# A batched matrix product: rounding x to float16 first and transposing it on TensorE as float32 words of two values

## Chip, cores and metric

One core of one Trainium2 chip. The metric is the device time in microseconds of one execution; "span" is the part of it that the profile covers (134.7 us of some 136.2).

## The reference

```python
batch, dim_i, dim_j, dim_k = 32, 256, 512, 384      # x: (32,256,512), y: (32,512,384), float32
def reference(x, y):
    return np.einsum('bij,bjk->bik', x, y).astype(np.float32)
```

## The kernel before

Four batches (Q = 4) form a group. A group of x arrives in one load of 2 MB, y and the output move per batch (768 KB and 384 KB). All loads and stores are issued by SyncE (SP) in program order. The multiplies of this kernel take x transposed, so it transposes x on TensorE first (256 transposes, 43.4 us of TensorE's busy time). It is transposed as float32 into PSUM (where this kernel's matrix products and transposes are written), and the eviction, the copy from there to SBUF (where its loaded tiles lie), rounds it to float16. A "bank" is in this text one PSUM tile of the transposes, `t_ps`, with 512 float32 words in each of 128 rows. y is rounded by ScalarE (ACT) and VectorE (DVE).

```python
    def transpose(q):                       # one group of four batches
        x_sb = x_of.pop(q)                  # [128, R=8 rows, J=512] float32
        xt_of[q] = xt_pool.tile([P, Q, NJ, NI, PQ, Q], MM_DT, name="xt_sb")
        n = 0
        for t in range(NJ):                 # NJ = 4
            for e in range(NI):             # NI = 2: eight PSUM banks per group
                t_ps = tpsum_pool.tile([P, Q, Q, PQ], F32, name="t_ps")
                for h in range(Q):          # four transposes fill one bank
                    keep(nc.tensor.transpose(
                            t_ps[:, h].rearrange("c g p -> c (g p)"),
                            x_sb[:, h * NI + e, t::NJ], identity))
                dst = xt_of[q][:, :, t, e].rearrange("c g p h -> c h g p")
                if n % 2 == 0: keep(nc.vector.tensor_copy(dst, t_ps))
                else:          keep(nc.scalar.copy(dst, t_ps))
                n += 1
    # ... load(b), round_y(b): 4 casts of 128x384, multiply(b): 8 matmuls, collect(b): 2 copies, store(b)
    for s in range(B + 2):
        if s + ahead < B:        load(s + ahead)
        if s >= 2:               collect(s - 2)
        if 1 <= s <= B:          multiply(s - 1)
        if s < B and s % Q == 0: transpose(s // Q)
        if s < B:                round_y(s)
        if s >= 2:               store(s - 2)
```

## Time and profile before

| | before |
|---|---|
| time, median of 4 runs (range) | 136.2 us (136.08 to 136.44) |
| bytes moved by the queue | 54.53 MB, 97.9% of the 16 DMA engines' span |
| TensorE / VectorE / ScalarE busy | 66% / 55% / 59% |
| last load of x lands, last eviction of its transposes ends | 115.2 us, 123.2 us |
| last store issued, span | 129.6 us, 134.7 us |

A busy share is an average over the whole span. What counts is the wait that ends last, so the prediction reads the transfer row and then the last 20 us.

### The profile page before, as it was taken

To read this page: it belongs to the slowest core of one execution; us is meant where nothing else is said; L and a number is where in the kernel's file an instruction comes from. 1 tells how busy PE (TensorE), PEld (TensorE's weight loads), DVE (VectorE), ACT (ScalarE), POOL (GpSimd) and SP (SyncE) were. 2 spreads that over 40 slices of the span, in tenths; PEclk is the share of its full clock that TensorE was granted. 3 is DMA by queue.
4 is the path that set the end of the run, shared out by engine and by line. 5 is a ranking of instruction groups with operands and counts; after the bars stand their busy time and mean duration, and the time that the engine had idled before them with its cause. 6 is when DMAs were issued, how large, how long until landed. Compare 5 with 4: busy or idle time off the path is not lost.

```text
span 134.7 us, 1539 instructions
## 1 busy us (share of the span) xinstructions
PE 89.5 (66%) x512; PEld 66.6 (49%) x512; DVE 73.7 (55%) x128; ACT 80.1 (59%) x129; POOL 0.7 (1%) x6
## 2 busy tenths in 40 slices
PE   0049499769677908949794983949459492794920
PEld 0048368644564408925492543936259360793510
DVE  0008855975397503873489340796228870378720
ACT  3007994996299602795479650699218990179910
POOL 2000000000000000000000000000000000000000
PEclk9999999999999985686999599599995999559995
DMA  5999999999999999999999999999999999999992
GB/s 131 399 413 423 447 412 416 416 434 414 404 422 451 425 399 424 421 435 437 400 416 430 438 425 410 421 418 454 407 409 425 433 440 402 421 421 413 412 410 84
DMA packets 10375, 54.62 MB, mean 405 GB/s; under 512 B 1152, under 2 KB 1152, under 8 KB 9344
## 3 DMA queue, kind: packets, MB, share of 16 engines
q1 hardware_dynamic: 10368, 54.53, 97.9%
q8 instruction: 4, 0.07, 0.2%
q14 instruction: 3, 0.02, 0.0%
HBM read 41.94 MB, written 12.58 MB: 405 GB/s over the span
## 4 chain that ended last, share of the span: by engine, by line
DMA 79%; PE 8%; ACT 5%; DVE 2%; issue 2%; SPq 1%; DVEq 0%
DMA y_sb<-in_y_dram 30%; DMA x_sb<-in_x_dram 27%; DMA out_dram<-o_sb 21%; PE o_ps L115 4%; PE t_ps L84 4%; ACT xt_sb L94 2%; ACT y_r L102 2%; DVE xt_sb L92 1%; DVE y_r L104 1%; DVE o_sb L130 0%; SPq L69 0%; ACT o_sb L128 0%; SPq L63 0%; DVEq L130 0%
## 5 line engine op out<-in xcount | busy, mean ns | idle before, releaser
L94 ACT CAST xt_sb<-t_ps 128x512 f16<-128x512 f32 x32 | 39.8, 1350 | 44.0 <-PE t_ps L84 43.9
L92 DVE CAST xt_sb<-t_ps 128x512 f16<-128x512 f32 x32 | 40.1, 1323 | 40.3 <-PE t_ps L84 40.2
L84 PE MATMUL t_ps<-identity,x_sb 128*128 128x128 f32 x256 | 43.4, 340 | 24.5 <-DMA x_sb<-in_x_dram 24.3
L115 PE MATMUL o_ps<-y_r,xt_sb 128*128 128x384 f16 x256 | 46.3, 342 | 14.9 <-ACT y_r L102 14.9
L84 PEld LDWEIGHTS t_ps<-identity,x_sb 128*128 128x128 f32 x256 | 41.1, 216 | 27.8 <-issue 26.4
L115 PEld LDWEIGHTS <-xt_sb 128*128 128x128 f16 x256 | 26.2, 102 | 34.2 <-issue 19.9
L102 ACT CAST y_r<-y_sb 128x384 f16<-128x384 f32 x64 | 30.2, 527 | 0.6 <-DMA y_sb<-in_y_dram 0.6
L130 DVE COPY o_sb<-o_ps 128x384 f32<-128x384 f32 x32 | 17.8, 556 | 15.1 <-PE o_ps L115 15.1
L104 DVE CAST y_r<-y_sb 128x384 f16<-128x384 f32 x64 | 19.9, 354 | 0.4 <-DMA y_sb<-in_y_dram 0.4
L128 ACT COPY o_sb<-o_ps 128x384 f32<-128x384 f32 x32 | 15.4, 483 | 3.8 <-PE o_ps L115 3.8
L94 ACT ACT_TABLE_LOAD x1 | 1.3, 1283 | 0.7 <-PEq L168 0.7
masks.py:199 POOL TENSOR_SCALAR_AFFINE_SELECT identity<-identity 128x128 f32<-128x128 f32 x1 | 0.3, 294 | 0.1
masks.py:197 POOL MEMSET identity<- 128x128 f32 x1 | 0.2, 205 | 0.3 <-POOLq L168 0.3
L168 POOL MEMSET const-bfloat16-1.0<- 128x1 bf16 x1 | 0.1, 102 | 0.0
L168 POOL MEMSET const-uint8-127<- 128x1 uint8 x1 | 0.1, 102 | 0.0
L168 POOL MEMSET const-float32-0.0<- 128x1 f32 x1 | 0.1, 99 | 0.2 <-issue 0.2
L168 POOL MEMSET const-float32-1.0<- 128x1 f32 x1 | 0.1, 99 | 0.0
## 6 DMA issues: line engine op xcount, KB each, us to landing
y_sb<-in_y_dram SPq DMA_DIRECT2D x32, 768.0 KB, 15.1
x_sb<-in_x_dram SPq DMA_DIRECT2D x8, 2048.0 KB, 14.2
out_dram<-o_sb SPq DMA_DIRECT2D x32, 384.0 KB, 14.1
```

What stands on the lines that cost most here:

```text
L84: nc.tensor.transpose(t_ps[:, h].rearrange("c g p -> c (g p)"), x_sb[:, h * NI + e, t::NJ], identity,)
L92: keep(nc.vector.tensor_copy(dst, t_ps))
L94: keep(nc.scalar.copy(dst, t_ps))
L102: keep(nc.scalar.copy(yr_of[b][:, t], y_sb[:, t]))
L104: keep(nc.vector.tensor_copy(yr_of[b][:, t], y_sb[:, t]))
L115: nc.tensor.matmul(ps_of[b][e], xt_sb[:, t, e].rearrange("c p h -> c (p h)"), y_r[:, t], start=(t == 0), stop=(t == NJ - 1),)
L128: keep(nc.scalar.copy(o_of[b][:, e], ps_of[b][e]))
L130: keep(nc.vector.tensor_copy(o_of[b][:, e], ps_of[b][e]))
L168: nc = _bacc.Bacc("TRN2", target_bir_lowering=False, num_devices=1)
```

## The change

The intent is to halve the transposes. x is rounded to float16 before it is transposed, and two neighbouring float16 values are taken together as one 32-bit word for TensorE's transpose. One transpose then carries two values per word, so a group needs 16 transposes instead of 32 and four PSUM banks instead of eight. A bank now holds 1024 values, and VectorE and ScalarE each evict half of it. The layout of the transposed x changes so that the two values of a word, and the four rows h, lie next to each other, and the multiply reads its weights with a step of two values.

```diff
         x_sb = x_of.pop(q)
-        xt_of[q] = xt_pool.tile([P, Q, NJ, NI, PQ, Q], MM_DT, name="xt_sb")
-        ... (32 transposes of x_sb, eight evictions, each of a whole bank, by the engines in turn)
+        x_r = xr_pool.tile([P, R, J], MM_DT, name="x_r")
+        for k in range(0, R, 2):
+            if k % 4 == 0:
+                keep(nc.vector.tensor_copy(x_r[:, k : k + 2], x_sb[:, k : k + 2]))
+            else:
+                keep(nc.scalar.copy(x_r[:, k : k + 2], x_sb[:, k : k + 2]))
+        x_w = x_r.bitcast(F32)
+        xt_of[q] = xt_pool.tile([P, NW, NI, Q * PQ, Q, 2], MM_DT, name="xt_sb")   # NW = 2
+        for n in range(NW):
             for e in range(NI):
-                ...
+                t_ps = tpsum_pool.tile([P, Q, Q * PQ], F32, name="t_ps")
                 for h in range(Q):
+                    keep(nc.tensor.transpose(t_ps[:, h], x_w[:, h * NI + e, n::NW], identity))
+                src = t_ps.bitcast(MM_DT).rearrange("c h (p w) -> c p h w", w=2)
+                half = slice(0, Q // 2), slice(Q // 2, Q)
+                dst = xt_of[q][:, n, e]
+                keep(nc.vector.tensor_copy(dst[:, :, half[0]], src[:, :, half[0]]))
+                keep(nc.scalar.copy(dst[:, :, half[1]], src[:, :, half[1]]))
 ... multiply(b):
-                        xt_sb[:, t, e].rearrange("c p h -> c (p h)"),
+                        xt_sb[:, t // 2, e, own, :, t % 2].rearrange("c p h -> c (p h)"),
```

More of the change, by code (lines that the diff above doesn't have):

```diff
@@ L40 @@
     PQ = P // Q
+    NW = NJ // 2
     const_pool = ctx.enter_context(tc.tile_pool(name="const", bufs=1))
     x_pool = ctx.enter_context(tc.tile_pool(name="x_pool", bufs=3))
+    xr_pool = ctx.enter_context(tc.tile_pool(name="xr_pool", bufs=2))
     y_pool = ctx.enter_context(tc.tile_pool(name="y_pool", bufs=10))
@@ L76, in transpose @@
         x_sb = x_of.pop(q)
-        xt_of[q] = xt_pool.tile([P, Q, NJ, NI, PQ, Q], MM_DT, name="xt_sb")
-        n = 0
-        for t in range(NJ):
+        x_r = xr_pool.tile([P, R, J], MM_DT, name="x_r")
[7 more added lines that the diff above has]
+        for n in range(NW):
             for e in range(NI):
-                t_ps = tpsum_pool.tile([P, Q, Q, PQ], F32, name="t_ps")
+                t_ps = tpsum_pool.tile([P, Q, Q * PQ], F32, name="t_ps")
                 for h in range(Q):
-                    keep(
-                        nc.tensor.transpose(
-                            t_ps[:, h].rearrange("c g p -> c (g p)"),
-                            x_sb[:, h * NI + e, t::NJ],
-                            identity,
-                        )
-                    )
-                dst = xt_of[q][:, :, t, e].rearrange("c g p h -> c h g p")
-                if n % 2 == 0:
-                    keep(nc.vector.tensor_copy(dst, t_ps))
-                else:
-                    keep(nc.scalar.copy(dst, t_ps))
-                n += 1
+                    keep(nc.tensor.transpose(t_ps[:, h], x_w[:, h * NI + e, n::NW], identity))
[4 more added lines that the diff above has]
+                keep(nc.scalar.copy(dst[:, :, half[1]], src[:, :, half[1]]))
     def round_y(b):
@@ L106, in multiply @@
     def multiply(b):
-        xt_sb, y_r = xt_of[b // Q][:, b % Q], yr_of.pop(b)
+        xt_sb, y_r = xt_of[b // Q], yr_of.pop(b)
+        own = slice(b % Q * PQ, (b % Q + 1) * PQ)
         ps_of[b] = [
```

## The prediction

> **What bounds the kernel now.** I read the page first, for the busy shares and the transfer row, and then the last 20 us of the timeline, because a change of compute can only show at the end of a kernel that is bound by transfers.
>
> ```profile
> PE 89.5 (66%) x512; PEld 66.6 (49%) x512; DVE 73.7 (55%) x128; ACT 80.1 (59%) x129; POOL 0.7 (1%) x6
> ...
> DMA  5999999999999999999999999999999999999992
> ...
> q1 hardware_dynamic: 10368, 54.53, 97.9%
> ...
> HBM read 41.94 MB, written 12.58 MB: 405 GB/s over the span
> ...
> DMA y_sb<-in_y_dram 30%; DMA x_sb<-in_x_dram 27%; DMA out_dram<-o_sb 21%; PE o_ps L115 4%; PE t_ps L84 4%; ACT xt_sb L94 2%; ACT y_r L102 2%; DVE xt_sb L92 1%; DVE y_r L104 1%; DVE o_sb L130 0%; SPq L69 0%; ACT o_sb L128 0%; SPq L63 0%; DVE
> ```
>
> No compute engine is busy for more than two thirds of the span. The 16 DMA engines are full in every slice but the first and the last, and the chain that ended last is 79% transfers by its engine line (30 + 27 + 21 in the lines shown, rounded). The 54.53 MB are inputs and outputs that every version has to move (41.94 MB in, 12.58 MB out). At the 413 to 430 GB/s that most middle slices show they need 127 to 132 us of the 134.7 us span.
>
> Next come the groups that the change touches, with the rounding of y as a yardstick for a plain cast:
>
> ```profile
> L94 ACT CAST xt_sb<-t_ps 128x512 f16<-128x512 f32 x32 | 39.8, 1350 | 44.0 <-PE t_ps L84 43.9
> L92 DVE CAST xt_sb<-t_ps 128x512 f16<-128x512 f32 x32 | 40.1, 1323 | 40.3 <-PE t_ps L84 40.2
> L84 PE MATMUL t_ps<-identity,x_sb 128*128 128x128 f32 x256 | 43.4, 340 | 24.5 <-DMA x_sb<-in_x_dram 24.3
> ...
> L102 ACT CAST y_r<-y_sb 128x384 f16<-128x384 f32 x64 | 30.2, 527 | 0.6 <-DMA y_sb<-in_y_dram 0.6
> L130 DVE COPY o_sb<-o_ps 128x384 f32<-128x384 f32 x32 | 17.8, 556 | 15.1 <-PE o_ps L115 15.1
> L104 DVE CAST y_r<-y_sb 128x384 f16<-128x384 f32 x64 | 19.9, 354 | 0.4 <-DMA y_sb<-in_y_dram 0.4
> L128 ACT COPY o_sb<-o_ps 128x384 f32<-128x384 f32 x32 | 15.4, 483 | 3.8 <-PE o_ps L115 3.8
> ```
>
> The evictions of the transposes idle for 40 us and more waiting for TensorE, and TensorE's transposes idle for 24 us waiting for x. That is slack, not cost: the whole line waits for transfers.
>
> The tail is where it could matter. The last group of x lands at 115.2 us. From the timeline of before:
>
> ```profile
> 115.29 6.61 PE L84 MATMUL t_ps<-identity,x_sb 128*128 128x128 f32 x32 [3.29 <-DMA x_sb<-in_x_dram]
> ...
> 120.69 2.55 ACT L94 CAST xt_sb<-t_ps 128x512 f16<-128x512 f32 x2 [0.40 <-PE t_ps L84]
> ...
> 123.61 5.36 PE L115 MATMUL o_ps<-y_r,xt_sb 128*128 128x384 f16 x32 [1.70 <-ACT y_r L102]
> ...
> 129.00 0.56 DVE L130 COPY o_sb<-o_ps 128x384 f32<-128x384 f32 x1 [0.74 <-PE o_ps L115]
> ```
>
> So x(7) takes 8.0 us from landing to its last eviction (115.2 to 123.24), the four batches multiply in 5.36 us, and the last copy ends at 129.56, with its store issued at 129.63. Is the transfer queue waiting for that store, or the store for the queue? The windows of the last microseconds answer it:
>
> ```profile
> 129.00:130.00 1.00, 0.00 (x0) 0.00 (x0) 0.56 (x1) 0.32 (x1) 0.00 (x0) 1.00 1.01 406
> 130.00:131.00 1.00, 0.00 (x0) 0.00 (x0) 0.00 (x0) 0.00 (x0) 0.00 (x0) 1.00 1.01 402
> 131.00:132.00 1.00, 0.00 (x0) 0.00 (x0) 0.00 (x0) 0.00 (x0) 0.00 (x0) 0.74 0.77 307
> 132.00:133.00 1.00, 0.00 (x0) 0.00 (x0) 0.00 (x0) 0.00 (x0) 0.00 (x0) 0.50 0.29 117
> ```
>
> The last two columns are DMA share and GB/s. At 129.63, the bytes still to move are 0.37 x 406 + 402 + 307 + 117 + 12 = 988 KB, of which the last store is 393 KB. So 595 KB, 1.4 us at 420 GB/s, lay ahead of it. The first load was issued at 0.74 us, and bytes flowed from about 1.5 us (213 KB in the second microsecond), so a store needs some 0.7 us to start. The slack of the last store is then about 1.4 - 0.7 = 0.7 us. If the tail's compute ends later than now by d, the kernel ends later by about d - 0.7. If it ends earlier, the gain is at most the half-empty 131 to 133 us: 307 + 117 KB took 2 us where full speed needs 1.0[...]. I put the most to be gained at 0.5 us.
>
> [...]today's evictions write single 2-byte values 8 bytes apart and take 1323 ns for 512 columns, while the contiguous copies from PSUM take 556 ns for 384. [...]in the tail the transposes run at a granted clock of 0.50 up to about 121 us and the multiplies at 1.00. In the group at 73.52 us the 32 multiplies took 6.99 us, because the first 11 started 0.32 us apart instead of 0.16.
>
> **The change part by part, per group of four batches.**
> - *Removed:* 16 of 32 transposes. In the tail 32 took 6.61 us, so 16 take 3.3 us at 0.21 us each. They lie beside other work except in the tail.
> - *Added:* four casts of 128x1024, two on each engine, between the landing of x and the transposes. Scaled from y's casts, VectorE needs at most 354 x 1024/384 = 944 ns and ScalarE at most 527 x 1024/384 = 1405 ns. Both are upper bounds[...]. Two on ScalarE are at most 2.8 us; I expect 2.0 us. This lies on the tail's path.
> - *Changed:* still eight evictions of 512 values each, now two halves of four banks. The writes become runs of four 2-byte values (8 bytes). If this gives the pace of the plain copies from PSUM, they cost at most 556 x 512/384 = 741 ns on VectorE and 644 ns on ScalarE, instead of 1323 and 1350. The reads now hop 512 bytes after each pair, which no row of before prices. I expect 0.6 to 0.75 us.
> - *Changed:* the multiply loads weights with a step of two values. I expect no cost: the loads hide behind multiplies, which are 0.16 us apart.
> - *Unmoved:* every transfer, its size and its order in the queue.
>
> Busy time per group: VectorE 73.7/8 = 9.2 us, less 4 x 1.32, plus 4 x 0.74, plus 2 x 0.94, is 8.8 us. ScalarE 10.0 us, less 5.4, plus 2.6, plus 2.8, is 10.0 us. One group's transfers (6.82 MB at 420 GB/s) take 16.2 us. So in the steady part nothing changes.
>
> The tail: x lands at 115.2, casts end at 117.2 (at most 118.0). The first bank is full 1.14 us later, as now (115.29 to 116.43): 118.4 (119.2). Three more banks follow at TensorE's pace of 0.85 us: 120.9 (121.7). The last bank is evicted by VectorE and then, if they must take turns, by ScalarE: 0.74 + 0.64 more, 122.3 (123.1). Today it is 123.24. The sum is a tail 0.1 to 0.9 us shorter, which is worth 0 to 0.5 us at the end.
>
> **The rivals.**
> 1. *The clock is cold.* Half as many transposes may not wake TensorE before the last multiplies. Then 5.36 us becomes about 7.0 us, as at 73.52: 1.6 us more. With the shorter tail that is 0.7 to 1.5 us late, less the slack of 0.7: +0 to +0.8 us, about 136.6. For it: activity falls from 6.6 to some 3.5 us.[...] I give it two in five.
> 2. *The evictions stay slow* (1.3 us, because of the hops in the read, in turns on each bank). Then the tail's evictions end at 119.2 + 4 x 1.35 + 1.32 = 125.9, 2.7 us late, and the end moves by 2.0 us: 138.2. With a cold clock too, 139.8.[...] Against it: the data move in whole words, in runs. One in eight.
> 3. *TensorE or the evictions limit the kernel now*, so that halving the transposes pays some per cent. The page speaks against it: DMA is full in 38 slices of 40. Below one in fifty.
>
> **Range and chances.** The likeliest end is where it is now: the gain of up to 0.5 us and the cold clock's loss of up to 0.8 us about cancel, so 136.2 us. The low end takes the whole gain and a little noise, 135.5; the high end most of rival 2, 137.8. To be over 2% slower the time must pass 138.9, which needs rival 2 with a cold clock: 6%. Over 2% faster is below 133.4 us, less than the transfers take: 1%. Within 2%: 93%.
>
> **What would show it right or wrong.** DMA share still 97 to 98% with 54.53 MB; 128 transposes instead of 256, with about 22 us of TensorE's busy time gone; x casts near 0.7 us (VectorE) and 1.05 us (ScalarE); evictions under 0.85 us; the last store issued between 128 and 131 us. The prediction is wrong if slices in the middle fall below full DMA (compute then starves the queue), if evictions exceed 1 us, or if the last store is issued after 132 us.

The tail's evictions came to 122.3 us (at most 123.1) against 123.24, so 0.1 to 0.9 us shorter, worth 0 to 0.5 us; against that stood rival 1's loss of up to 0.8 us; together 136.2 us. Rival 1 and rival 2: their chances, two in five and one in eight, were my estimates.

Estimates of mine were also the 2.0 us for two casts on ScalarE and the paces of 0.7 and 1.05 us (under the 944 and 1405 ns scaled from y's casts), the lower end of 0.6 us for an eviction (under the 741 ns scaled from the plain copies), that the two engines might have to take turns on a bank, and that TensorE's clock follows how long it has worked. On the last, the trace of before shows only this: in the tail the granted clock was 0.50 up to 121.0 us, 0.77 from 121.0 to 121.5 and 1.00 from 121.5 to 122.0, all while transposes ran. That casts scaled by their size are upper bounds no view of before shows, but the runs do: x's casts are 2.67 times as large as y's and took 1.95 times as long on VectorE (689 against 354 ns) and 1.98 times on ScalarE (1043 against 527).

## The result, and the profile after

The changed kernel takes 136.2 us (median of 4 runs, 136.06 to 136.40), the kernel before 136.2 us. The outputs are right. The ratio is 0.9999, with a 95% interval of 0.998 to 1.0018. Ratios here are the mean time of one kernel's fast runs over that of the other's of the same rounds, so they are not quite the ratio of the medians.

From the page of the changed kernel: busy shares, transfer row, and the groups that the change touched. The lines of before stand in the prediction.

```profile
PE 78.7 (58%) x384; PEld 50.8 (38%) x384; DVE 58.2 (43%) x144; ACT 75.7 (56%) x145; POOL 0.7 (1%) x6
...
DMA  5999999999999999999999999999999999999992
...
q1 hardware_dynamic: 10368, 54.53, 98.1%
...
L93 PE MATMUL t_ps<-identity,x_r 128*128 128x128 f32 x128 | 29.8, 402 | 33.0 <-DVE x_r L84 31.1
...
L86 ACT CAST x_r<-x_sb 128x1024 f16<-128x1024 f32 x16 | 15.9, 1043 | 28.4 <-DMA x_sb<-in_x_dram 28.2
L98 ACT COPY xt_sb<-t_ps 128x512 f16<-128x512 f16 x32 | 18.3, 587 | 12.9 <-DVE xt_sb L97 12.8
...
L84 DVE CAST x_r<-x_sb 128x1024 f16<-128x1024 f32 x16 | 10.3, 689 | 30.0 <-DMA x_sb<-in_x_dram 30.0
...
L97 DVE COPY xt_sb<-t_ps 128x512 f16<-128x512 f16 x32 | 13.6, 425 | 18.2 <-PE t_ps L93 17.9
```

In a group's line the columns are busy us, mean ns of one, then idle us before the group and what ended most of it. All compute engines have less to do: VectorE 15.5 us less, TensorE 10.8, ScalarE 4.4. The evictions fell from 1323 to 425 ns (VectorE) and from 1350 to 587 ns (ScalarE). The transfer row is the same to the byte. The idle times name the reason: VectorE and ScalarE spent 30 and 28 us waiting for x to land before they could round it. The work that was saved became waiting for transfers.

The tail of the changed kernel, from its timeline:

```profile
114.82 1.99 ACT L86 CAST x_r<-x_sb 128x1024 f16<-128x1024 f32 x2 [3.07 <-DMA x_sb<-in_x_dram]
...
115.67 1.00 PE L93 MATMUL t_ps<-identity,x_r 128*128 128x128 f32 x3 [2.96 <-DVE x_r L84]
...
116.87 2.94 PE L93 MATMUL t_ps<-identity,x_r 128*128 128x128 f32 x13 [0.20 <-ACT x_r L86]
...
120.31 0.58 ACT L98 COPY xt_sb<-t_ps 128x512 f16<-128x512 f16 x1 [0.16 <-DVE xt_sb L97]
...
121.36 4.06 PE L119 MATMUL o_ps<-y_r,xt_sb 128*128 128x384 f16 x24 [1.54 <-ACT y_r L105]
...
125.18 0.93 ACT L105 CAST y_r<-y_sb 128x384 f16<-128x384 f32 x2 [0.68 <-DMA y_sb<-in_y_dram]
...
127.25 0.56 DVE L134 COPY o_sb<-o_ps 128x384 f32<-128x384 f32 x1 [0.93 <-PE o_ps L119]
...
127.87 0.33 SPq L139 DMA_DIRECT2D out_dram<-o_sb  x1
```

From the landing of x to the last eviction it is now 6.1 us (114.82 to 120.89) where it was 8.0. The halved transposes account for it: they run from 115.67 to 119.81, 4.1 us instead of 6.6, while the first casts put 0.85 us in front. The multiplies run at full clock (granted 1.00 in the windows from 120 to 128 us). The last batch even has to wait for its y to land (125.18), and the last store is issued at 127.87 instead of 129.63, 1.8 us earlier. The windows of the end (last columns: granted clock, DMA share, GB/s) show what became of these 1.8 us:

```profile
129.00:130.00 1.00, 0.00 (x0) 0.00 (x0) 0.00 (x0) 0.00 (x0) 0.00 (x0) 0.90 1.05 416
130.00:131.00 1.00, 0.00 (x0) 0.00 (x0) 0.00 (x0) 0.00 (x0) 0.00 (x0) 0.50 1.01 402
131.00:132.00 1.00, 0.00 (x0) 0.00 (x0) 0.00 (x0) 0.00 (x0) 0.00 (x0) 0.50 0.76 304
132.00:133.00 1.00, 0.00 (x0) 0.00 (x0) 0.00 (x0) 0.00 (x0) 0.00 (x0) 0.50 0.34 135
```

These are nearly the rates of before: 416, 402, 304 and 135 against 406, 402, 307 and 117. I call the two half-empty microseconds from 131 to 133 the taper. The engines are idle for the last 7 us, and the queue drains as it did.

### The profile page after: what moved, and what is told of

It reads as the page before. It is cut to its first block, busy times and chain, and to the rows that moved or that the text cites. A ratio compares the mean times of both kernels' runs of the same rounds, so it can differ in the third digit from the quotient of the medians.

```text
span 134.6 us, 1310 instructions
## 1 busy us (share of the span) xinstructions
PE 78.7 (58%) x384; PEld 50.8 (38%) x384; DVE 58.2 (43%) x144; ACT 75.7 (56%) x145; POOL 0.7 (1%) x6
## 3 DMA queue, kind: packets, MB, share of 16 engines
q1 hardware_dynamic: 10368, 54.53, 98.1%
## 4 chain that ended last, share of the span: by engine, by line
DMA 89%; ACT 2%; SPq 2%; PE 1%; issue 0%; DVE 0%; ACTq 0%
DMA y_sb<-in_y_dram 34%; DMA out_dram<-o_sb 31%; DMA x_sb<-in_x_dram 24%; SPq L72 1%; ACT x_r L86 1%; PE o_ps L119 1%; DVE o_sb L134 0%; ACT y_r L105 0%; SPq L66 0%; SPq L139 0%; ACTq L105 0%
## 5 line engine op out<-in xcount | busy, mean ns | idle before, releaser
L119 PE MATMUL o_ps<-y_r,xt_sb 128*128 128x384 f16 x256 | 48.8, 351 | 15.5 <-ACT y_r L105 15.4
L93 PE MATMUL t_ps<-identity,x_r 128*128 128x128 f32 x128 | 29.8, 402 | 33.0 <-DVE x_r L84 31.1
L119 PEld LDWEIGHTS <-xt_sb 128*128 128x128 f16 x256 | 27.0, 105 | 37.2 <-DVE o_sb L134 12.4
L93 PEld LDWEIGHTS t_ps<-identity,x_r 128*128 128x128 f32 x128 | 24.1, 216 | 38.8 <-issue 33.2
L105 ACT CAST y_r<-y_sb 128x384 f16<-128x384 f32 x64 | 29.7, 517 | 4.6 <-DMA y_sb<-in_y_dram 4.6
L86 ACT CAST x_r<-x_sb 128x1024 f16<-128x1024 f32 x16 | 15.9, 1043 | 28.4 <-DMA x_sb<-in_x_dram 28.2
L98 ACT COPY xt_sb<-t_ps 128x512 f16<-128x512 f16 x32 | 18.3, 587 | 12.9 <-DVE xt_sb L97 12.8
L84 DVE CAST x_r<-x_sb 128x1024 f16<-128x1024 f32 x16 | 10.3, 689 | 30.0 <-DMA x_sb<-in_x_dram 30.0
L97 DVE COPY xt_sb<-t_ps 128x512 f16<-128x512 f16 x32 | 13.6, 425 | 18.2 <-PE t_ps L93 17.9
```

The lines of the kernel that those rows point to most:

```text
L84: keep(nc.vector.tensor_copy(x_r[:, k : k + 2], x_sb[:, k : k + 2]))
L86: keep(nc.scalar.copy(x_r[:, k : k + 2], x_sb[:, k : k + 2]))
L93: keep(nc.tensor.transpose(t_ps[:, h], x_w[:, h * NI + e, n::NW], identity))
L97: keep(nc.vector.tensor_copy(dst[:, :, half[0]], src[:, :, half[0]]))
L98: keep(nc.scalar.copy(dst[:, :, half[1]], src[:, :, half[1]]))
L105: keep(nc.scalar.copy(yr_of[b][:, t], y_sb[:, t]))
```

## The experiments

Two questions stayed. Is the change worth anything on the engines, and which part of it? And how much later or earlier may the tail's compute end before the time moves? The first was asked with "light" kernels. They load only three groups of x and eight batches of y and use them again, so their results are wrong, and 25 MB are left to move. The edit, made to the kernel before and to the changed one:

```diff
-        if b % Q == 0:
+        if b % Q == 0 and b // Q < 3:
             x_of[b // Q] = x_pool.tile(...)          # and its load
+        if b >= 8:
+            return
         y_of[b] = y_pool.tile(...)                   # and its load
-        x_sb = x_of.pop(q)
+        x_sb = x_of[q % 3]
-        y_sb = y_of.pop(b)
+        y_sb = y_of[b % 8]
```

### light_before and light_after

> Wrong results on purpose: only the first three x tiles and the first eight y tiles are loaded and then used again; every store stays. 25 MB are left to move instead of 54.5, some 60 us at 420 GB/s, so the engines should set the time. Theory (transfers hide the change): the kernel gets much faster than 136 us, about 100 to 110 us (per group of four batches some 5.5 us of transposes and evictions, 1 us of rounding, 5.4 us of multiplies, 12 us in all, eight times, plus start and end), because nothing but transfers held it at 136. Rival (the engines also hold it near 136 us, so that transfers and engines are about balanced): over 125 us.

> The changed kernel with the same cut in loads (wrong results on purpose). Theory: the change does make the engines' work shorter, and only the transfers hide it, so this beats light_before by about 10 to 15% (90 to 95 us): 2.0 us of casts added, 2 to 3 us of transposes and about 3 us of evictions saved per group. Rival (gain and cost of the change cancel on the engines themselves, and hiding has nothing to do with it): within 2% of light_before.

Measured: light_before 111.9 us (110.44 to 112.0), ratio to the kernel before 0.818 (interval 0.813 to 0.824). light_after 99.98 us (99.23 to 101.63), ratio 0.733 (0.728 to 0.739). Their quotient is 0.733/0.818 = 0.896. The change makes the engines' work 10% shorter once transfers no longer hide it, at the near end of what was expected; the estimate of light_after's time (90 to 95 us) was too low. Both rivals fall: the engines alone need 112 us, not 136, and gain and cost don't cancel on them. From TensorE's timelines, one group's multiplies, the next group's transposes, and its multiplies:

```profile
52.80 5.36 PE L117 MATMUL o_ps<-y_r,xt_sb 128*128 128x384 f16 x32 [1.85 <-ACT y_r L104]
58.00 4.46 PE L86 MATMUL t_ps<-identity,x_sb 128*128 128x128 f32 x32
64.31 5.36 PE L117 MATMUL o_ps<-y_r,xt_sb 128*128 128x384 f16 x32 [1.85 <-ACT y_r L104]
```

```profile
48.59 5.36 PE L121 MATMUL o_ps<-y_r,xt_sb 128*128 128x384 f16 x32 [1.57 <-ACT y_r L107]
53.99 2.78 PE L95 MATMUL t_ps<-identity,x_r 128*128 128x128 f32 x16
58.34 5.36 PE L121 MATMUL o_ps<-y_r,xt_sb 128*128 128x384 f16 x32 [1.57 <-ACT y_r L107]
```

The first fence is light_before: 11.5 us per group. The second is light_after: 9.75 us. The multiplies take 5.36 us in both; the transposes shrink from 4.46 to 2.78 us and the wait before the multiplies from 1.85 to 1.57. What held light_before up can be read from the chain of work that ended last (58 to 82 us): 45% of it are multiplies, 34% VectorE's evictions, and only 6% transposes. In light_after (48 to 69 us) 84% of the chain is ScalarE's work. One group's transfers take 16.2 us (6.82 MB at 420 GB/s). At this pace the engines had 4.7 us of slack per group before, and have 6.4 after. That is where the gain went: off the path, into slack that was there already. In the full kernels I estimate the slack to be smaller: their mean granted clock is 0.89 and 0.83, against 0.999 and 0.982 in these two profiles, and some groups' 32 multiplies took 6.99 and 7.04 us (before) and 6.74 to 7.25 us (after) instead of 5.36.

### light_f16x32: round first, but no pairs

```diff
+    identity_h = const_pool.tile([P, P], MM_DT); nc.vector.tensor_copy(identity_h, identity)
+        x_r = ...                                    # the four casts of the change
-                t_ps = tpsum_pool.tile([P, Q, Q, PQ], F32, name="t_ps")
+                t_ps = tpsum_pool.tile([P, Q, Q, PQ], MM_DT, name="t_ps")
-                            x_sb[:, h * NI + e, t::NJ], identity,
+                            x_r[:, h * NI + e, t::NJ], identity_h,
```

> Half of the change alone, with the cut loads (wrong results on purpose): x is rounded first, but transposed as 32 transposes of single float16 values per group, into float16 PSUM tiles, and evicted with the old scattered writes. If what makes the evictions cheap is the run of adjacent values that pairing allows, evictions stay near 1.3 us and this is slower than light_before by the casts, 5 to 15%. If it is the 16-bit source alone, evictions fall to about 0.5 us and this is near light_after.

Measured: 125.8 us (123.55 to 127.16; two of the four runs count as slow, the fast ones took 123.55 and 125.28), ratio of the fast runs to the kernel before 0.913 (0.905 to 0.920), so 0.913/0.818 = 1.115 times light_before: 11.5% slower. Its profile was taken in a slow run, so I use only its durations, beside those of light_before's profile, which was a fast run. light_f16x32, then light_before:

```profile
L103 DVE COPY xt_sb<-t_ps 128x512 f16<-128x512 f16 x32 | 38.0, 1334 | 6.6 <-PE t_ps L95 6.6
L105 ACT COPY xt_sb<-t_ps 128x512 f16<-128x512 f16 x32 | 38.2, 1387 | 4.7 <-PE t_ps L95 4.7
```

```profile
L96 ACT CAST xt_sb<-t_ps 128x512 f16<-128x512 f32 x32 | 38.7, 1394 | 24.3 <-PE t_ps L86 24.3
...
L94 DVE CAST xt_sb<-t_ps 128x512 f16<-128x512 f32 x32 | 38.7, 1344 | 20.7 <-PE t_ps L86 20.7
```

A 16-bit source makes the evictions no cheaper at all (1334 against 1344 ns, 1387 against 1394). Rounding first, alone, is a loss. But the casts are not shown to be its cause, as I had expected. From TensorE's timeline of the same profile:

```profile
43.76 7.04 PE L126 MATMUL o_ps<-y_r,xt_sb 128*128 128x384 f16 x32 [2.21 <-ACT y_r L113]
...
57.47 7.48 PE L126 MATMUL o_ps<-y_r,xt_sb 128*128 128x384 f16 x32 [1.70 <-ACT y_r L113]
```

A group takes 13.7 us, 2.2 more than in light_before, and the multiplies, partly at half clock, take 1.7 to 2.1 of them: from 57.47 us the first 13, by their weight loads, start 0.32 us apart, as in the kernel before from 73.5 to 76.7 us, where the granted clock was 0.50. The fast runs have no profile; their mean granted clock (0.88 and 0.90, against 0.96 to 1.00 in light_before) points the same way.

### light_scatter: pairs, but the old writes

```diff
-        xt_of[q] = xt_pool.tile([P, NW, NI, Q * PQ, Q, 2], MM_DT, name="xt_sb")
+        xt_of[q] = xt_pool.tile([P, NW, NI, 2, Q * PQ, Q], MM_DT, name="xt_sb")
-                src = t_ps.bitcast(MM_DT).rearrange("c h (p w) -> c p h w", w=2)
+                src = t_ps.bitcast(MM_DT).rearrange("c h (p w) -> c w h p", w=2)
-                dst = xt_of[q][:, n, e]
+                dst = xt_of[q][:, n, e].rearrange("c w p h -> c w h p")
-                        xt_sb[:, t // 2, e, own, :, t % 2].rearrange("c p h -> c (p h)"),
+                        xt_sb[:, t // 2, e, t % 2, own].rearrange("c p h -> c (p h)"),
```

> light_after (cut loads, wrong results on purpose) with the paired transposes kept, 16 per group, but evicted with the old scattered writes: single values 8 bytes apart, the two values of a word going to two planes. Separates the two things that pairing brings. If the cheap evictions are what pays, they go back to about 1.33 us on VectorE and 1.39 us on ScalarE and the kernel loses most of its lead: 112 us or more. If the halved number of transposes pays, it stays within 3% of light_after's 100 us.

Measured: 138.8 us (138.24 to 139.11), ratio to the kernel before 1.018 (1.015 to 1.021). With the number of transposes still halved it is 1.018/0.733 = 1.39 times light_after, and slower than light_before too (1.018/0.818 = 1.24; these quotients join two batches of runs, each measured against its own runs of the kernel before). From its page and its timeline:

```profile
L100 ACT COPY xt_sb<-t_ps 128x512 f16<-128x512 f16 x32 | 37.6, 1296 | 14.7 <-DVE xt_sb L99 14.7
L99 DVE COPY xt_sb<-t_ps 128x512 f16<-128x512 f16 x32 | 37.7, 1326 | 7.7 <-PE t_ps L95 7.7
```

```profile
70.70 2.78 PE L95 MATMUL t_ps<-identity,x_r 128*128 128x128 f32 x16
...
73.43 4.69 ACT L100 COPY xt_sb<-t_ps 128x512 f16<-128x512 f16 x4 [1.83 <-DVE xt_sb L99]
...
78.49 1.76 PE L121 MATMUL o_ps<-y_r,xt_sb 128*128 128x384 f16 x5 [5.01 <-ACT y_r L107]
```

The evictions are back at 1.3 us. I expected 112 us or more, and the loss is far larger, for two reasons that the timeline shows. The 16 transposes end at 73.5, but ScalarE starts its first half of a bank only when VectorE is done with the other (it waits 1.83 us for that), and ends its four at 78.1; TensorE then stands idle for 5.0 us. After that pause the first multiplies of these groups run at half clock (0.32 us apart), and 32 of them took 8.04 us in the group before, where light_after needs 5.36. The reads changed as well here (single values 4 bytes apart), but light_f16x32 read in runs and needed the same 1.33 us, so the writes are to blame.

Two groups of light_scatter take 30.7 us (multiplies starting at 62.62 and 93.28), 15.3 each, 5.6 more than in light_after. The longer wait before the multiplies is 3.4 of them (5.0 against 1.57) and their half clock 2.1 (8.04 and 6.95 against 5.36). So the halved transposes alone don't pay: they take 2.78 us here too, but with slow evictions TensorE waits for what it saved, and more. It is the writes in runs that let the gain through, which fits the share of the evictions in light_before's chain.

Three things are not shown. How much the halving adds is open, as no run had 32 transposes and short evictions. Such a run might need no pairing: in the old layout h lies innermost too, and only the order of the old copies scatters the writes. Nor does this run show that halving hurts: the old evictions alternated over whole banks, while here both engines take turns on each bank (ScalarE waits 1.83 us for VectorE). And half-clock multiplies came in light_f16x32 too, with all 32 transposes, so halving is not shown to be their cause.

### light_order: reads in runs instead of writes

```diff
+                dst, src = dst.rearrange("c p h w -> c h p w"), src.rearrange("c p h w -> c h p w")
-                keep(nc.vector.tensor_copy(dst[:, :, half[0]], src[:, :, half[0]]))
-                keep(nc.scalar.copy(dst[:, :, half[1]], src[:, :, half[1]]))
+                keep(nc.vector.tensor_copy(dst[:, half[0]], src[:, half[0]]))
+                keep(nc.scalar.copy(dst[:, half[1]], src[:, half[1]]))
```

> light_after with the same bytes evicted in another order: h outermost, so that the PSUM reads are contiguous and the SBUF writes are pairs of two values 16 bytes apart, instead of reads that hop and runs of four values written. If writes are what hopping costs most, VectorE's eviction rises from 0.425 us to about 0.8 us and ScalarE's from 0.585 to 0.7 or more, and the kernel is up to 3% slower than light_after. If reads cost more, the evictions get cheaper.

Measured: 101.5 us (100.81 to 103.32), ratio 0.743 (0.738 to 0.748), so 0.743/0.733 = 1.013 times light_after; the two intervals just meet, so the 1.3% is likely rather than certain. Its evictions:

```profile
L101 ACT COPY xt_sb<-t_ps 128x512 f16<-128x512 f16 x32 | 17.8, 628 | 10.3 <-DVE xt_sb L100 10.3
L100 DVE COPY xt_sb<-t_ps 128x512 f16<-128x512 f16 x32 | 17.2, 625 | 9.3 <-PE t_ps L95 9.3
```

The same bytes go to the same places. Written in pairs of values 16 bytes apart they cost 625 ns on VectorE and 628 on ScalarE; written in runs of four, with reads that hop 512 bytes after each pair, 425 and 587. Here the hops in the SBUF write cost more than those in the PSUM read, 200 ns on VectorE and 41 on ScalarE. I had guessed 0.8 and 0.7 us or more.

### light_alt: whole banks, no turns

```diff
-                keep(nc.vector.tensor_copy(dst[:, :, half[0]], src[:, :, half[0]]))
-                keep(nc.scalar.copy(dst[:, :, half[1]], src[:, :, half[1]]))
+                if e % 2 == 0: keep(nc.vector.tensor_copy(dst, src))
+                else:          keep(nc.scalar.copy(dst, src))
```

> light_after with each bank evicted whole by one engine, alternating (two on VectorE, two on ScalarE per group), so that the two engines never take turns on one bank. In the profile after ScalarE waited 12.8 us for VectorE's half. If taking turns costs on the engines' path, this is 1 to 3% faster than light_after; if TensorE's transposes set the pace there, the same within 1%, or slower because a whole bank on ScalarE takes some 1.0 us against TensorE's 0.85 us per bank.

Measured: 99.0 us (98.76 to 100.07), ratio 0.729 (0.724 to 0.734). It ran in another batch than light_after (0.733, 0.728 to 0.739), and the intervals overlap, so no difference is shown. With evictions this short, no cost of taking turns is shown (0.733 with turns, 0.729 without). The expectation's 1.0 us for a whole bank on ScalarE was an estimate (twice the 587 ns of half a bank in the profile after is 1.17 us); its time is not given here. With light_scatter's long ones ScalarE waited 1.83 us per group for it, but no run tried those without turns.

### after_late4, after_late10, before_late4: how late may the last store be?

```diff
-                keep(nc.vector.tensor_copy(o_of[b][:, e], ps_of[b][e]))
+                for _ in range(5 if b == B - 1 else 1):      # 11 in after_late10
+                    keep(nc.vector.tensor_copy(o_of[b][:, e], ps_of[b][e]))
```

> The changed kernel, with the last copy of the last batch done 5 times instead of once on VectorE (the same values into the same place, so the result stays right): the last store comes some 2.1 us later than 127.9, at about 130.0. Theory (the transfers still queued set the end; in the profile after, 1345 KB lay ahead of the last store, 3.2 us, less 0.7 us to start, so 2.5 us of slack): no change, within 0.3 us of 136.2. Rival (the last store's time sets the end): +2.1 us, 138.3.

> The same with 11 copies: the last store some 5.3 us later, at about 133.2. Theory: the slack of 2.5 us is used up, and the end moves by about 2.8 us, 139.0. Rival (last store sets the end): +5.3 us, 141.5. If it stays at 136.2 there is more slack than the bytes say.

> The kernel before with the last copy done 5 times: last store at about 131.7 instead of 129.6. Theory: its slack was 0.7 us, so the end moves by about 1.4 us, 137.6. Rival: no slack, +2.1 us; or as much slack as the changed kernel, no change.

All three kernels give the right result. The last store's time comes from one profiled run each, the time from all fast runs:

| kernel | last store issued | later by | ratio to before (interval) | time later by |
|---|---|---|---|---|
| changed kernel | 127.87 us | | 0.9999 (0.998 to 1.002) | |
| after_late4 | 130.4 | 2.6 us | 1.001 (0.999 to 1.004) | 0.1 us, not clear of zero |
| after_late10 | 135.15 | 7.3 us | 1.026 (1.021 to 1.032) | 3.6 us |
| kernel before | 129.63 | | | |
| before_late4 | 131.7 | 2.1 us | 1.005 (1.001 to 1.009) | 0.7 us |

The last column is the ratio less one, times 136.2. The idea of slack holds: delay costs little up to some point and is paid beyond it. Its size was too small in my sums. after_late10 leaves 7.3 - 3.6 = 3.7 us of slack for the changed kernel where I had 2.5, and before_late4 leaves 2.1 - 0.7 = 1.4 us for the kernel before where I had 0.7 (by the intervals of the ratios alone, 2.9 to 4.5 and 0.9 to 2.0). I had expected 139.0 us of after_late10 and 137.6 of before_late4; they took 140.1 and 136.8. after_late10's last store was expected at 133.2: ten more copies took 5.9 us and not 5.3, and another 1.4 came from the last 32 multiplies, which ran partly at half clock in its profiled run (7.18 us). A likely reason for the larger slack is in the windows of after_late10. Its last store was alone in the queue:

```profile
135.00:136.00 1.00, 0.00 (x0) 0.00 (x0) 0.09 (x1) 0.00 (x0) 0.00 (x0) 0.50 0.04 15
136.00:137.00 1.00, 0.00 (x0) 0.00 (x0) 0.00 (x0) 0.00 (x0) 0.00 (x0) 0.50 0.95 378
```

Alone, it moves its 393 KB in about one microsecond. In the unchanged tail the last 424 KB or more take two (131 to 133 us). By this reading a late store can fill that taper, and only the rest of its delay is added to the end. My sum had not counted on that. This fits the three runs; no run tested it alone.

### scatter_full: the prediction's second rival, made real

The edit of light_scatter on the changed kernel, with all loads and a right result.

> The same scattered evictions in the changed kernel with all its loads and a right result: this is rival 2 of the prediction made real (evictions of 1.3 us in turns on each bank). By the prediction's sum it would be 138.2 us. By what was measured since (evictions end about 3.1 us later than in the changed kernel, against a slack that late10 put at about 3.4 us by its end) it should be within 0.6 us of 136.2.

Measured: 137.8 us (137.26 to 138.71), ratio 1.011 (1.008 to 1.015). My later expectation (within 0.6 us of 136.2) was wrong; the prediction's 138.2 was closer, though by another way. It had reckoned only the tail. The timeline shows that the engines have no slack left between groups:

```profile
117.00 1.99 ACT L86 CAST x_r<-x_sb 128x1024 f16<-128x1024 f32 x2
117.26 1.28 DVE L84 CAST x_r<-x_sb 128x1024 f16<-128x1024 f32 x2
...
125.89 6.96 PE L119 MATMUL o_ps<-y_r,xt_sb 128*128 128x384 f16 x32 [5.02 <-ACT y_r L105]
```

No wait for x stands behind the casts any more: the engines were still busy with the group before. In the full kernel groups follow each other every 15.6 us (multiplies starting at 48.45 and 95.16, three groups apart), against 16.2 us of transfers. The first multiplies start at 17.49 us and the last end at 132.9, and the queue runs dry before (its share is 0.06 from 129 to 130 us). The last multiplies start 4.5 us later than in the changed kernel. light_scatter took 138.8 us with most of the loads cut, so the engines, not the transfers, set this time.

### after_start and after_onact: what is left at the two ends

```diff
+        eng = nc.scalar if b < 3 else nc.sync                # after_start
-        keep(nc.sync.dma_start(out=y_of[b], ...
+        keep(eng.dma_start(out=y_of[b], ...
-ON_ACT = ()                                                  # after_onact
+ON_ACT = (28, 29, 30, 31)
```

> A try at what is left: the DMA engines move little between 2.0 and 3.5 us although five transfers are queued or being issued one after another by SyncE (0.4 to 0.6 us each). The first three y loads are issued by ScalarE instead. If the serial issue starves the start, the span falls by up to 1 us, 0.7%. If the start is limited by the transfers themselves, no change within 0.2%.

> The last four stores are issued from ScalarE instead of SyncE, where they don't queue behind the stores that wait for a free place. If the half-empty last two microseconds come from stores issued too late or in line, the end comes up to 0.5 us earlier (0.4%). If they come from DMA engines that finish their shares at different times, no change within 0.2%.

Measured: after_start 135.94 us, ratio 0.998 (0.996 to 1.000); after_onact 136.19 us, ratio 0.999 (0.997 to 1.000). Issuing the first loads from two engines gives some 0.2%, which is not clear of nothing. Issuing the last stores from ScalarE changes nothing, and the taper stays (261 and 129 GB/s in its windows from 131 to 133 us). Whether single DMA engines finish at different times no view here shows, so the taper's cause is left open. No version that keeps all loads beat the two kernels by a clear margin.

## Why the prediction was right, point by point

- **Transfers bound the kernel:** right, and now tested. 54.53 MB and 98.1% after; with the loads cut, the same programs take 112 and 100 us. The centre of 136.2 us owes something to luck: it was a balance of up to 0.5 us gained and up to 0.8 us lost at the end, and neither came.
- **128 transposes fewer, about 22 us of TensorE's busy time gone:** wrong in size. The transposes' busy time fell by 13.6 us (43.4 to 29.8), and that of the multiplies rose by 2.5 us (46.3 to 48.8). The prediction simply halved. But 16 transposes took 2.78 us in light_after where 32 took 4.46 in light_before, with a mean granted clock of 0.982 and 0.999 in these profiles: the four that fill a group's first bank need one cast each, so they come one by one (the first three take 1.0 us in the tail). And TensorE ran at a lower clock: the mean granted clock fell from 0.89 to 0.83.
- **Casts near 0.7 and 1.05 us:** right (689 and 1043 ns).
- **Evictions of 0.6 to 0.75 us:** still too dear; 425 ns on VectorE and 587 on ScalarE.
- **Weights with a step of two at no cost:** right. A load of weights shows 105 ns after and 102 before, and 32 multiplies at full clock take 5.36 us in both.
- **Engines take turns on a bank:** they do here (ScalarE waited 12.8 us for VectorE's halves in all), at no cost that light_alt could show.
- **A tail shorter by 0.1 to 0.9 us:** the direction was right. From landing to last eviction it is 1.9 us shorter, because 16 transposes take 4.1 us where 32 took 6.6. It is 1.0 us shorter than the sum of 7.1, for two reasons. The sum let all casts end (2.0 us) before the first transpose, but the transposes began 0.85 us after x landed, and three of the first four lay beside the casts, so that the first bank's eviction started 0.6 us sooner than in the sum; and what follows the last transpose took 1.1 us instead of 1.4. The last store then came at 127.87 us, just below the range of 128 to 131 that I gave, and TensorE had still waited 0.33 us for y's last load, which landed at 125.1 us and which I had not looked at.
- **Worth 0 to 0.5 us at the end:** measured zero. The taper that I counted as possible gain stayed as it was when the last store came 1.8 us earlier.
- **Slack of 0.7 us:** mis-sized; about 1.4 us (before_late4).
- **Rival 1, a cold clock:** it came in three groups in the middle (7.23, 6.74 and 7.25 us for 32 multiplies; the kernel before had two of 7.04 and 6.99), where slack took it. That it stayed away from the tail was luck of the run: of the five profiles that share the changed kernel's multiplies (with after_late4, after_late10, after_start and after_onact), the one of after_late10 has it there, with 7.18 us. How long TensorE has to work before the clock rises these runs don't tell: in the tail of before the half clock lasted some 6 us, through transposes alone (115.29 to about 121.2), and in the tail of the changed kernel the granted clock was 0.54 from 116 to 118 us, 0.61 from 118 to 120 and 1.00 from 120, with only 4.1 us from the first transpose to the last.
- **Rival 2, slow evictions:** did not come (425 and 587 ns where it had 1.3 us), and scatter_full shows that it would have cost 1.1%, by engines behind in every group and not by the tail alone. **Rival 3** is refuted by the result.
- **Readings that were off without moving the result:** 18 of the 38 middle slices of before lie within 413 to 430 GB/s, not most (their mean is 421). And 133.4 us is not less than the 127 to 132 us that the prediction gave the transfers.

## What to carry to other kernels

Here the transfer queue was full from start to end, and making the engines faster bought slack and nothing else. Before such a change, work out what the last store has ahead of it in the queue; before crediting a change with a gain, run it with most of the loads cut, and vary its parts one at a time. When transposed data are evicted, look at the writes first: with the same 16 transposes per group, single values 8 bytes apart made the light kernel 39% slower than runs of four. For 512 float16 values from PSUM to SBUF the runs show: single values 8 bytes apart 1323 to 1344 ns on VectorE and 1296 to 1394 on ScalarE, pairs 16 bytes apart 625 and 628, runs of four 425 and 587. Look at the clock too: in light_scatter, after waits of 5.0 us, TensorE came back at half clock, and 32 multiplies took 6.89 to 8.04 us instead of 5.36. That the wait is the cause is not shown: in the changed kernel multiplies of 6.74 to 7.25 us came after waits of 1.5 us.
